# Two early weight slabs, states in a kept order, and scaled tiles evicted by ACT

## The chip, the cores and the metric

The kernel runs on one core of a Trainium2 chip. The metric is device time in microseconds of one execution; lower is better. The engines that matter are PE (TensorE, matrix products), DVE (VectorE), ACT (ScalarE), POOL (GpSimd) and SP (SyncE, which here only issues DMAs). Each works through its own list of instructions in order; semaphores make one engine wait for another.

## The reference

One inference step of one hybrid decoder layer, for a prompt of 512 positions and 8 samples of 4 positions, all in float32:

```
n = RMSNorm(h);  z = n @ w_in            # q | k | v | gate | gMLP u | v | branch gates A | B
q, k = rotary(q), rotary(k) * DK**-0.5   # 4 heads, DK 256, DV 512
o, s_new = retention_chunked(q, k, v, s0)
y_a = silu(gate) * rmsnorm(o, g_ret)     # the norm is by head
y_b = gelu(u) * spatial_gating(layernorm(gelu(v)))
h = h + (sigmoid(zga) * (y_a @ w_br_a) + sigmoid(zgb) * (y_b @ w_br_b)) @ w_o
h = h + square(relu(rmsnorm(h) @ w_up)) @ w_down
h = h + sigmoid(rmsnorm(h) @ w_pg) * (p @ w_pp)
```

The outputs are the normed h of all positions, the new retention states of prompt and samples, and the samples' gMLP rows.

## The kernel before

Activations lie transposed: a tile has 128 features as partitions and 544 columns (512 prompt positions, 32 sample positions). A weight slab is 128 x 1024 float32, 512 KB, and holds what one tile of 128 output features needs (8 blocks of 128 x 128).

Float32 products are made of three products of a cheaper type. `split` writes a value's high part (`hi`, a cast on ACT, L123) and its remainder (`lo`, a subtraction on DVE, L124, which reads `hi`). Weights and activations are both split, and a block's product is hi·hi + hi·lo + lo·hi. `dense` (L304) issues a tile's products: 8 blocks, 3 products, 2 halves of 272 columns, 48 matmuls into one `Product`, a pair of PSUM banks called `f`. There are two such pairs, used in turn, so a tile's first matmul waits until the tile two before it has been read out of PSUM.

`Feed` brings the weights. A list of jobs is planned beforehand; `load` issues slab loads on SP while one of 4 raw buffers is free, and `wide` splits a raw slab into one of 3 `hl` buffers. The first two slabs come differently: `begin(2)` sets them aside and `piece(i)` loads them in quarters between the 8 loads of the input `xT`, so that PE can start early.

Head 0 makes the query tiles q0 and q1 together (`first_two`), from activations scaled by the norm's weights but not yet by 1/rms, because the rms is not known yet. The squares (L473) and their sum (L474), kept in program order by `pin`, give `r1`. `copied` takes a product out of PSUM by ACT (L602). `times_r1` takes it out by DVE and multiplies by `r1` on the way (L596); it serves the two key tiles k0, k1 and the first two value tiles v0, v1 of head 0. From v2 on the activations themselves are normalised (L619, eight tiles, split again), so plain copies do. Then come v3 and four gate tiles. Heads 1 to 3 have the same tiles, and between a head's keys and values stands the branch-A product of the head before (`branch_a`, `ya` being its gated and normed output: `group_normed`, the multiplication in L880 and then a split).

Around the dense tiles lies the attention work of the head as small "chores" that fall due some ticks later: key and value transposes on PE (`kt`, `vt`, and `vs` for the sample rows, fed by a copy on POOL, L900), scores, `state_ahead` (loads a sample's 256 x 512 state by SP, L806, into one of 5 buffers, and splits it), `sample_state` (products with it), `prompt_output`, `group_norm` (a ones-product on PE, a square root on ACT, a reciprocal on DVE, L491).

The order of each engine's instructions is not the order of the code. A scheduler goes through a modelled timeline when the program is built and fixes one list for each engine; instructions under `pin` keep their order among themselves. At run time nothing overtakes.

Of the kernel before, what the change touches and what calls it, by code (L numbers as in the profile page):

```python
# [11 lines left out]
ALU = mybir.AluOpType  # L12
# [45 lines left out]
class Slots:  # L58
# [11 lines left out]
    def get(self, dtype=F32):  # L70
        i = self.free.popleft()
        self.count += 1
        t = self.pools[i].tile([P, T], dtype, tag=f"s{i}", name=f"s{i}_{self.count}")
        self.where[id(t)] = (i, t)
        return t
# [7 lines left out]
def halves(ap):  # L83
    return ap.rearrange("p (a b) -> p a b", a=2)


def layer(tc, a, o):
    nc = tc.nc
    act, dve, pool, pe = nc.scalar, nc.vector, nc.gpsimd, nc.tensor
    with ExitStack() as ctx:  # L90
# [9 lines left out]
        get, put = slots.get, slots.put  # L100
# [21 lines left out]
        def split(hi, lo, src):  # L122
            act.copy(hi, src)  # L123
            dve.tensor_tensor(out=lo, in0=src, in1=hi.bitcast(F32), op=ALU.subtract)  # L124

        class Feed:
# [35 lines left out]
            def piece(self, i):  # L162
                c, d = (slice(i * SLAB // 4 + e, (i + 1) * SLAB // 4 + e) for e in (0, SLAB))
                for t, hl, src in self.first:
                    nc.sync.dma_start(t[:, c], src[:, c])
                for t, hl, src in self.first:
                    split(hl[:, c], hl[:, d], t[:, c])
                if i == 3:
                    self.busy -= len(self.first)

            def load(self):
                while self.jobs:
# [101 lines left out]
        feed = Feed()  # L274
# [8 lines left out]
        def bank(name="m"):  # L283
            return psm[-1].tile([P, 512], F32, tag="m", name=name)
# [28 lines left out]
        def tile_of(xs):  # L313

            w = feed.take()
            ps = Product()
            dense(ps, [(*at(w, k * P), *xs[k]) for k in range(KD)])
            return ps
# [147 lines left out]
        pin = tc.keep_in_program_order  # L466
# [27 lines left out]
        def scaled_split(src, g):  # L494

            hi, lo = get(F32R), get(F32R)
            act.activation(hi, src, AF.Copy, scale=g)
            dve.scalar_tensor_tensor(
                out=lo, in0=src, scalar=g, in1=hi.bitcast(F32), op0=ALU.mult, op1=ALU.subtract
            )  # L500
            return hi, lo
# [48 lines left out]
        ps = bank("warm")  # L550
# [5 lines left out]
        def g(base, k):  # L556
            return gcols[:, base + k : base + k + 1]
# [3 lines left out]
        for k in range(KD):  # L561
            t = get()
            nc.sync.dma_start(t, a["xT"][k * P : (k + 1) * P, :])
            xs_raw.append(t)
            xs.append(scaled_split(t, g(G_MIX, k)))
            if k % 2 == 0:
                feed.piece(k // 2)
        total = get()
        for k in range(KD):
            add_square(total, xs_raw[k], k == 0, pin)  # L570
# [13 lines left out]
        r1s = {}  # L584
# [7 lines left out]
            return tile_of(xs)  # L592

        def times_r1(ps):
            t = get()
            dve.tensor_tensor(out=halves(t), in0=ps.all, in1=halves(r1s["r"]), op=ALU.mult)  # L596
            return t


        def copied(ps):  # L600
            t = get()
            act.copy(halves(t), ps.all)  # L602
            return t
# [197 lines left out]
        def state_ahead(c, b):  # L801

            km = hp.tile([96, DK], F32R, tag="km", name="km", bufs=2)
            act.activation(km, c.k3.bitcast(F32), AF.Copy, scale=maskb[:, b : b + 1])  # L804
            raw = hp.tile([P, 2, DV], F32, tag="state", name="state", bufs=STATES)
            nc.sync.dma_start(raw, a["state"][b, c.h].rearrange("(i p) v -> p i v", i=2))  # L806
            parts = []
            for i in range(2):
                hi, lo = get(F32R), get(F32R)
                split(hi[:, :DV], lo[:, :DV], raw[:, i])  # L810
                parts.append((hi, lo))
            c.states[b] = km, raw, parts
# [75 lines left out]
        def values(c):  # L888
            c.vh = hp.tile([P, 4, DV], F32R, tag="vh", name="vh")
            c.vl = hp.tile([P, 4, DV], F32R, tag="vl", name="vl")  # L890
            c.pvs = bank("vs")
            for m2 in range(2):
                if c.h == m2 == 0:
                    t2 = [times_r1(next_in()) for _ in range(2)]
                    renew()
                else:
                    t2 = pair()
                for i, t in enumerate(t2):
                    r = hp.tile([P, 96], F32, tag="v96", name="v96", bufs=2)
                    pool.tensor_copy(  # L900
                        r.rearrange("p (a s) -> p a s", a=3), t[:, None, LP:].to_broadcast([P, 3, NS])
                    )
                    later(VALUES[i], lambda m=2 * m2 + i, t=t, r=r: values_by_token(c, m, t, r))
# [14 lines left out]
        for h in range(H):  # L918
            c = Head()
            c.h = h  # L920
            head_tables(c)
            r = None
            if h == 0:
                q = [copied(ps) for ps in first_two(xs, [(k,) for k in range(KD)])]
                start_norm()
                r = r1s["r"]
                chores([(2 * j, normalise, j) for j in range(KD)])
                k = [times_r1(next_in()) for _ in range(2)]
            else:
                q = pair()  # L930
                k = pair()
# [17 lines left out]
            for b in range(NB):  # L949
                plan += [(AHEAD[b], state_ahead, c, b), (STATE[b], sample_state, c, b)]  # L950
# [185 lines left out]
        for m in range(KD):  # L1136
            ps, t = tile_of(yb), get()
# [163 lines left out]
        for s in range(2):  # L1301
# [3 lines left out]
            for i in range(0, KD, 2):  # L1305
# [15 lines left out]
                t, sq = get(), get()  # L1321
# [5 lines left out]
                for j, (t1, sq1, m) in enumerate(x2):  # L1327
                    for c0, c1 in quarters[2:] if end and j else ((s * TH, (s + 1) * TH),):
                        c, p = slice(c0, c1), slice(c0 - s * TH, c1 - s * TH)
                        if end:  # L1330
                            ps = todo[0] if j else area
# [16 lines left out]
                else:  # L1348
                    dve.tensor_tensor(
                        out=squares[:, :TH], in0=squares[:, :TH], in1=squares[:, TH:], op=ALU.add  # L1350
# [140 lines left out]
```

## Time and profile before

| what | value |
|---|---|
| median of 3 runs | 1263.17 us (1261.87 to 1264.41) |
| the profiled execution, its own time | 1260.18 us |
| its span, first to last instruction | 1258.4 us |
| PE busy, of the span | 98% |
| DVE, ACT, POOL busy | 70%, 50%, 7% |
| mean granted clock of PE | 0.996 |
| DMA | 176.27 MB, 140 GB/s on average |

The profile gives, for one execution, the busy time of each engine, who waited for whom, and the instructions in order of time. A row of the timeline reads: start, length, engine and line, operation, tile written <- tiles read, count, and in brackets the idle time before it and what ended that. Rows that follow each other with the same work are merged ("x48"). Matmuls are pipelined: one lasts 0.289 us in the records, and the next starts about 0.127 us after it. SP rows are DMA issues, not transfers.

### The profile page before, as it was taken

To read this page: it belongs to the slowest core of one execution; us is meant where nothing else is said; L and a number is where in the kernel's file an instruction comes from. 1 tells how busy PE (TensorE), PEld (TensorE's weight loads), DVE (VectorE), ACT (ScalarE), POOL (GpSimd) and SP (SyncE) were. 2 spreads that over 40 slices of the span, in tenths; PEclk is the share of its full clock that TensorE was granted. 3 is DMA by queue.
4 is the path that set the end of the run, shared out by engine and by line. 5 is a ranking of instruction groups with operands and counts; after the bars stand their busy time and mean duration, and the time that the engine had idled before them with its cause. 6 is when DMAs were issued, how large, how long until landed. Compare 5 with 4: busy or idle time off the path is not lost.

```text
span 1258.4 us, 22939 instructions
## 1 busy us (share of the span) xinstructions
PE 1236.8 (98%) x9432; PEld 1206.0 (96%) x9432; DVE 887.0 (70%) x1297; ACT 630.3 (50%) x1047; POOL 92.6 (7%) x127
## 2 busy tenths in 40 slices
PE   8999999999999999999999999999999999999996
PEld 8989999999999998999999999999999999999995
DVE  7976854686468655767678654559459879888966
ACT  6453553443434353643455532446248568577733
POOL 0201100110010001010000000000000001000000
PEclk9999999999999999999999999999999999999998
DMA  9328323822263225653546453222546667665302
GB/s 313 112 94 273 104 78 103 280 92 87 92 247 122 85 70 202 212 160 92 129 135 187 141 202 93 85 84 91 127 114 162 173 173 180 186 163 149 122 18 71
DMA packets 65336, 176.27 MB, mean 140 GB/s; under 512 B 7408, under 2 KB 10736, under 8 KB 65232
## 3 DMA queue, kind: packets, MB, share of 16 engines
q1 hardware_dynamic: 54288, 135.42, 32.6%
q0 software_dynamic: 10944, 39.39, 13.4%
q8 instruction: 74, 1.21, 0.4%
q14 instruction: 30, 0.25, 0.1%
HBM read 153.55 MB, written 21.23 MB: 139 GB/s over the span
## 4 chain that ended last, share of the span: by engine, by line
PE 53%; DVE 2%; ACT 2%; DMA 1%; issue 0%; DVEq 0%; ACTq 0%
PE f L304 20%; PE fa L390 16%; PE f L390 12%; PE pg L304 4%; DVE hl L124 1%; PE sp L1081 1%; ACT hl L123 1%; DMA raw<-in_w_down 0%; PE norm L486 0%; DVE s L491 0%; DVE s L124 0%; DMA raw<-in_w_pg 0%; PE sp L1082 0%; PE gt L968 0%; DVE s L880 0%
## 5 line engine op out<-in xcount | busy, mean ns | idle before, releaser
L304 PE MATMUL f<-s,hl 128*128 128x272 f32 x5088 | 674.0, 289 | 4.5 <-ACT hl L123 1.8
L304 PEld LDWEIGHTS f<-s,hl 128*128 128x128 f32 x5088 | 655.2, 188 | 12.5 <-ACT hl L123 2.2
L124 DVE TENSOR_TENSOR hl<-raw,hl 128x1024 fp32r<-128x1024 f32 (+2 forms) x259 | 288.8, 1123 | 107.3 <-ACT hl L123 105.1
L123 ACT CAST hl<-raw 128x1024 fp32r<-128x1024 f32 (+2 forms) x259 | 249.1, 969 | 177.2 <-PE f L304 99.0
L390 PE MATMUL fa<-s,hl 128*128 128x272 f32 x1728 | 238.9, 289 | 2.0 <-ACT hl L123 1.0
L390 PEld LDWEIGHTS fa<-s,hl 128*128 128x128 f32 x1728 | 224.3, 188 | 4.2 <-ACT hl L123 1.6
L390 PE MATMUL f<-s,hl 128*128 128x272 f32 x1296 | 183.5, 288 | 1.7 <-DVE s L409 1.1
L390 PEld LDWEIGHTS f<-s,hl 128*128 128x128 f32 x1296 | 170.1, 188 | 3.1 <-DVE s L409 2.0
L123 ACT CAST s<-s 128x544 fp32r<-128x544 f32 (+4 forms) x170 | 97.4, 598 | 48.0 <-DVE s L765 12.2
L124 DVE TENSOR_TENSOR s<-s,s 128x544 fp32r<-128x544 f32 (+4 forms) x170 | 108.6, 659 | 6.4 <-ACT s L123 5.7
L826 DVE SCALAR_TENSOR_TENSOR state<-state,su 128x512 f32<-128x512 f32 x64 | 43.8, 685 | 38.1 <-PE su L825 38.0
L123 ACT CAST s<-state 128x512 fp32r<-128x512 f32 x64 | 37.9, 621 | 38.4 <-DMA state<-in_state 18.7
L124 DVE TENSOR_TENSOR s<-state,s 128x512 fp32r<-128x512 f32 x64 | 42.8, 687 | 19.8 <-ACT s L123 16.7
L417 ACT ACTIVATE s<-fa 128x272 f32<-128x272 f32 x36 | 14.3, 398 | 64.5 <-PE fa L390 64.5
L602 ACT COPY s<-f 128x544 f32<-128x544 f32 x28 | 17.2, 614 | 48.8 <-PE f L304 48.6
L491 DVE RECIPROCAL s<-s 128x544 f32<-128x544 f32 (+1 forms) x9 | 28.6, 3176 | 10.0 <-ACT s L489 10.0
L193 POOL DMA_DIRECT2D raw<-in_w_up x12 | 10.3, 854 | 311.3 <-DVE s L124 189.4
L304 PE MATMUL pg<-s,s 128*128 128x272 f32 x240 | 30.7, 288 | 0.0
L804 ACT ACTIVATE km<-k,maskb 96x256 fp32r<-96x256 f32 x32 | 15.9, 508 | 29.3 <-PE su L825 28.6
L830 POOL DMA_DIRECT2D out_state_s<-state x32 | 23.0, 719 | 101.2 <-DVE state L826 101.2
L304 PEld LDWEIGHTS pg<-s,s 128*128 128x128 f32 x240 | 30.3, 188 | 0.1
L464 PE MATMUL o<-s,vh 128*128 128x256 f32 (+2 forms) x128 | 30.3, 324 | 0.0
(179 smaller groups left out, 1128.7 us busy)
## 6 DMA issues: line engine op xcount, KB each, us to landing
raw<-in_w_in SPq DMA_DIRECT2D x66, 512.0 KB, 3.3
state<-in_state SPq DMA_DIRECT2D x32, 512.0 KB, 4.8
out_state_s<-state POOLq DMA_DIRECT2D x32, 512.0 KB, 4.7
raw<-in_w_up SPq DMA_DIRECT2D x20, 512.0 KB, 3.3
raw<-in_w_down SPq DMA_DIRECT2D x20, 512.0 KB, 3.3
raw<-in_w_in SPq DMA_DIRECT2D x36, 256.0 KB, 3.2
raw<-in_w_up SPq DMA_DIRECT2D x36, 256.0 KB, 3.3
raw<-in_w_down SPq DMA_DIRECT2D x36, 256.0 KB, 3.4
```

The costliest lines, as they stand in the source:

```text
L123: act.copy(hi, src)
L124: dve.tensor_tensor(out=lo, in0=src, in1=hi.bitcast(F32), op=ALU.subtract)
L304: pe.matmul(ps.p[s], w, x[:, s * TH : (s + 1) * TH], start=first and i == 0 and j == 0, stop=last and i == n - 1 and j == 2, skip_group_ch ...
L390: pe.matmul(ps, a_, b_, start=first and k == j == 0, stop=k == 3 and j == 2, skip_group_check=True)
L417: act.activation(t1[:, hi_half], pa, AF.Copy, scale=-1.0)
L464: pe.matmul(ps[:rows, c], u, v, start=i == 0 and j == 0, stop=i == n - 1 and j == 2)
L491: dve.reciprocal(r[:, c], r[:, c])
L602: act.copy(halves(t), ps.all)
L804: act.activation(km, c.k3.bitcast(F32), AF.Copy, scale=maskb[:, b : b + 1])
L826: dve.scalar_tensor_tensor(out=raw[:, i], in0=raw[:, i], scalar=gamma**LS, in1=ps, op0=ALU.mult, op1=ALU.add)
L830: pool.dma_start(o["state_s"][b, c.h].rearrange("(i p) v -> p i v", i=2), raw)
L1081: pe.matmul(ps[:, j * P : (j + 1) * P], gvt[j][m // 4][:, cols], wst[:, m], start=True, stop=True)
```

## The change

Three edits. First, a new method `begun` is called when the input loads have all been issued: it runs `load` at once, so two more slabs (the third and fourth, for k0 and k1) are asked for on SP ahead of the tables (`cos`, `sin`, five small ones, `dtab`, `qmask`). Only then are the first two raw buffers given back; `piece` no longer does this. Second, the state loads of head 0 are put under `pin`. Third, `times_r1` takes the product out of PSUM by ACT (`copied`) and multiplies by `r1` in SBUF on DVE.

```diff
                 for t, hl, src in self.first:
                     split(hl[:, c], hl[:, d], t[:, c])
-                if i == 3:
-                    self.busy -= len(self.first)
+
+            def begun(self):
+
+                self.load()
+                self.busy -= len(self.first)
...
             if k % 2 == 0:
                 feed.piece(k // 2)
+        feed.begun()
         total = get()
...
         def times_r1(ps):
-            t = get()
-            dve.tensor_tensor(out=halves(t), in0=ps.all, in1=halves(r1s["r"]), op=ALU.mult)
+            t = copied(ps)
+            dve.tensor_tensor(out=t, in0=t, in1=r1s["r"], op=ALU.mult)
             return t
...
-            nc.sync.dma_start(raw, a["state"][b, c.h].rearrange("(i p) v -> p i v", i=2))
+            load = nc.sync.dma_start(raw, a["state"][b, c.h].rearrange("(i p) v -> p i v", i=2))
+            if c.h == 0:
+                pin(load)
```

The lists of the engines that the scheduler makes of this differ up to the scores of head 1, some 1200 matmuls in; from there on they hold the same instructions in the same order. Line numbers of the new kernel are 3 to 5 higher. Three places matter for what follows.

SP, at the start. `s` tiles filled from `in_xT` are the input, `raw` of 128x1024 a whole slab. Before:

```order
L563 DMA s_22_164<-in_xT 128x544
L572 DMA s_33_193<-in_cos 128x544
L573 DMA s_34_194<-in_sin 128x544
L580 DMA st_dec<-in_st_dec 128x16
L580 DMA sts<-in_sts 96x4
L580 DMA maskb<-in_maskb 96x8
L580 DMA dsam<-in_dsam 96x128
L580 DMA fold<-in_fold 64x32
L665 DMA dtab<-in_dtab 128x640
L667 DMA qmask<-in_qmask 128x256
L185 DMA raw<-in_w_in 128x1024 x4
L806 DMA state<-in_state 128x2x512 x5
```

Now:

```order
L188 DMA raw<-in_w_in 128x1024 x2
L576 DMA s_33_197<-in_cos 128x544
L577 DMA s_34_198<-in_sin 128x544
L584 DMA st_dec<-in_st_dec 128x16
L584 DMA sts<-in_sts 96x4
L584 DMA maskb<-in_maskb 96x8
L584 DMA dsam<-in_dsam 96x128
L584 DMA fold<-in_fold 64x32
L668 DMA dtab<-in_dtab 128x640
L670 DMA qmask<-in_qmask 128x256
L188 DMA raw<-in_w_in 128x1024 x11
L809 DMA state<-in_state 128x2x512 x2
```

Two slabs moved ahead of nine tables, and the five first states moved from behind the sixth slab of the kernel to behind the fifteenth and later.

ACT, from the last square of the first norm on. `s_35` and `s_36` are q0 and q1 out of PSUM, `s_42` and `s_47` are k0 and k1, `s_37` is r1, and each cast to `hl` is the high part of the next slab. Before:

```order
L473 ACTIVATE s_32_190<-s_22_164 128x544
L602 COPY s_35_327<-f 128x544
L123 CAST hl<-raw 128x1024
L602 COPY s_36_329<-f 128x544
L123 CAST hl<-raw 128x1024 x2
L489 ACTIVATE s_37_331<-norm,eps 128x272 x2
L123 CAST hl<-raw 128x1024
L123 CAST s_38_351<-s_1_98 128x544
L123 CAST s_40_380<-s_4_110 128x544
L123 CAST hl<-raw 128x1024
```

Now:

```order
L476 ACTIVATE s_32_194<-s_22_164 128x544
L123 CAST hl<-raw 128x1024
L605 COPY s_35_327<-f 128x544
L123 CAST hl<-raw 128x1024
L605 COPY s_36_329<-f 128x544
L123 CAST hl<-raw 128x1024
L492 ACTIVATE s_37_331<-norm,eps 128x272 x2
L605 COPY s_42_408<-f 128x544
L123 CAST hl<-raw 128x1024
L123 CAST s_38_351<-s_1_98 128x544
L123 CAST s_40_380<-s_4_110 128x544
L605 COPY s_47_475<-f 128x544
```

The third slab's cast moved ahead of the copy of q0, and the copies of k0 and k1 are new. On DVE the multiplications of k0, k1, v0, v1 stand where they stood.

ACT, at the keys of head 1. `s_137` and `s_143` are its query tiles, `s_148` and `s_149` its keys k0 and k1; `s_139`, `s_141`, `s_144`, `s_146` are the high parts of `ya` of head 0, which PE reads in the first product after k1 (`branch_a`). Before:

```order
L123 CAST s_139_1532<-s_103_999 128x544
L123 CAST s_141_1549<-s_113_1131 128x544
L123 CAST s_144_1574<-s_128_1279 128x544
L123 CAST s_146_1591<-s_133_1381 128x544
L602 COPY s_148_1631<-f 128x544
L123 CAST hl<-raw 128x1024
L123 CAST s_161_1819<-s_137_1491 128x544
L123 CAST s_163_1824<-s_143_1565 128x544
L123 CAST s_166_1829<-s_165_1828 128x8x32
L602 COPY s_149_1687<-f 128x544
L123 CAST hl<-raw 128x1024
```

Now:

```order
L605 COPY s_148_1635<-f 128x544
L123 CAST hl<-raw 128x1024
L123 CAST s_163_1828<-s_143_1569 128x544
L123 CAST s_166_1833<-s_165_1832 128x8x32
L605 COPY s_149_1691<-f 128x544
L123 CAST hl<-raw 128x1024
L123 CAST s_139_1536<-s_103_1003 128x544
L123 CAST s_141_1553<-s_113_1135 128x544
L123 CAST s_144_1578<-s_128_1283 128x544
L123 CAST s_146_1595<-s_133_1385 128x544
```

The four casts of `ya` moved from ahead of the copy of k0 to behind the copy of k1 and one slab's cast.

DVE, at the same place. `s_138` is 1/rms of the group norm, made by the reciprocal; `s_140`, `s_142`, `s_145`, `s_147` are the low parts of `ya`. Before:

```order
L491 RECIPROCAL s_138_1499<-s_138_1499 128x544
L634 TENSOR_TENSOR s_158_1770<-s_143_1565,s_34_194 128x544
L880 TENSOR_TENSOR s_103_999<-s_103_999,s_138_1499 128x544
L880 TENSOR_TENSOR s_113_1131<-s_113_1131,s_138_1499 128x544
L880 TENSOR_TENSOR s_128_1279<-s_128_1279,s_138_1499 128x544
L880 TENSOR_TENSOR s_133_1381<-s_133_1381,s_138_1499 128x544
L124 TENSOR_TENSOR hl<-raw,hl 128x1024
L635 TENSOR_TENSOR s_143_1565<-s_143_1565,s_33_193 128x544
L636 TENSOR_TENSOR s_137_1491<-s_137_1491,s_158_1770 128x544
L124 TENSOR_TENSOR s_140_1533<-s_103_999,s_139_1532 128x544
```

Now, the reciprocal standing six instructions ahead of the first row:

```order
L885 TENSOR_TENSOR s_103_1003<-s_103_1003,s_138_1503 128x544
L885 TENSOR_TENSOR s_113_1135<-s_113_1135,s_138_1503 128x544
L885 TENSOR_TENSOR s_128_1283<-s_128_1283,s_138_1503 128x544
L885 TENSOR_TENSOR s_133_1385<-s_133_1385,s_138_1503 128x544
L686 TENSOR_TENSOR s_167_1837<-qs,qmask 128x256
L124 TENSOR_TENSOR s_164_1829<-s_143_1569,s_163_1828 128x544
L124 TENSOR_TENSOR s_166_1833<-s_165_1832,s_166_1833 128x8x32
L636 TENSOR_TENSOR s_148_1635<-s_148_1635,s_33_197 128x544
L637 TENSOR_TENSOR s_150_1699<-s_149_1691,s_34_198 128x544
L124 TENSOR_TENSOR hl<-raw,hl 128x1024
L124 TENSOR_TENSOR s_140_1537<-s_103_1003,s_139_1536 128x544
```

Between the reciprocal and the first low part of `ya` stood 8 instructions, 1 of them on a slab; now 15 stand there: 2 of them are on slabs, and 3 read k0 or k1.

PE's list at that place has the 48 matmuls of k1 and then, with nothing between, the products with `s_139`, then `s_140`. In head 0, PE's transposes of v0 and v1 (`vt`, `vs`) stood 12 and 45 matmuls into v2 (the first `vs` 18); now they stand 4 and 25 matmuls into v3.

## The prediction

> **What bounds the kernel.** I read the page's busy shares first, then busy times by stretch, then who waited for whom, then the timeline at the places that the new lists touch.
>
> ```profile
> PE 1236.8 (98%) x9432; PEld 1206.0 (96%) x9432; DVE 887.0 (70%) x1297; ACT 630.3 (50%) x1047; POOL 92.6 (7%) x127
> ```
>
> PE is busy 98% of the span. The change neither adds nor removes a matmul, so it can only win what PE idles in the stretch it touches, and lose by making PE idle anew.
>
> ```profile
> 20.00:25.00 5.00, 3.58 (x26) 3.37 (x27) 4.13 (x5) 3.49 (x4) 0.00 (x0) 1.00 0.97 366
> ...
> 40.00:50.00 10.00, 8.73 (x68) 8.34 (x67) 10.00 (x16) 3.25 (x4) 1.62 (x1) 1.00 0.16 52
> 50.00:60.00 10.00, 9.74 (x78) 9.28 (x77) 10.00 (x16) 5.20 (x9) 6.91 (x7) 1.00 0.31 107
> 60.00:80.00 20.00, 20.00 (x157) 19.65 (x156) 17.48 (x32) 13.87 (x26) 0.97 (x2) 1.00 0.23 73
> 80.00:100.00 20.00, 20.00 (x118) 16.68 (x117) 11.45 (x18) 5.99 (x11) 3.82 (x6) 1.00 0.53 174
> 100.00:120.00 20.00, 20.00 (x133) 18.38 (x132) 14.30 (x21) 8.57 (x16) 3.59 (x5) 1.00 0.83 268
> ```
>
> Columns: stretch, length, then busy us of PE, weight loads, DVE, ACT, POOL, then PE's granted clock, DMA share, GB/s. PE loses 1.4 us in 20 to 25 and 1.5 us in 40 to 60, where DVE is full (10.00 of 10) and ACT half empty; from 60 on it loses nothing.
>
> ```profile
> PE f L304 <- ACT hl L123: 1.8, 2, 1.6
> ...
> PE f L304 <- DVE s L596: 1.3, 2, 0.7
> ```
> ```profile
> L777 PE MATMUL vs<-ident,v 128*96 128x128 f32 x16 | 4.4, 278 | 0.3
> ```
>
> The waits are those the edits aim at: a slab's cast, and `times_r1` on DVE (L596). 0.3 us more are `vs` transposes waiting for POOL's copy of v.
>
> **The change, part by part.** Idle time counts from the modelled end of the last matmul, 0.29 us after its start, while the next would normally start after 0.13: each gap costs 0.16 more than it shows.
>
> *Early slabs.*
>
> ```profile
> 14.92 3.94 ACT L473 ACTIVATE s<-s 128x544 f32<-128x544 f32 x7
> 15.59 4.87 DVE L474 TENSOR_TENSOR s<-s,s 128x544 f32<-128x544 f32 x6 [0.29 <-ACT s L473]
> 15.88 1.86 SPq L185 DMA_DIRECT2D raw<-in_w_in  x4
> ...
> 18.75 0.59 ACT L602 COPY s<-f 128x544 f32<-128x544 f32 x1
> 19.83 1.04 ACT L123 CAST hl<-raw 128x1024 fp32r<-128x1024 f32 x1 [0.48 <-DMA raw<-in_w_in]
> ...
> 20.91 1.23 DVE L124 TENSOR_TENSOR hl<-raw,hl 128x1024 fp32r<-128x1024 f32 x1 [0.44 <-ACT hl L123]
> 20.93 0.77 PE L304 MATMUL f<-s,hl 128*128 128x272 f32 x4 [1.61 <-ACT hl L123]
> ...
> 22.19 3.17 PE L304 MATMUL f<-s,hl 128*128 128x272 f32 x23 [0.49 <-DVE hl L124]
> ```
>
> The slab now lands well before ACT is through its squares, so the DMA wait is gone. But ACT still ends the squares first: cast 18.8 to 19.8, then the copy of q0 to 20.4, which k0 needs as well, since it takes q0's place in PSUM. PE can start k0 at 20.45. After 4 matmuls it needs `lo`, and DVE's six additions last until 20.46: `lo` ends at 21.65 instead of 22.15. PE's fifth matmul comes at 21.65 instead of 22.19: **0.54 us won**, not the 2.4 us of both gaps. Bounds: 0 and 2.4. The tables land later by two slabs' time; the first is read by rotary, behind eight normalisations, so that costs nothing while DVE is this late.
>
> *Eviction by ACT.*
>
> ```profile
> 41.61 6.28 PE L304 MATMUL f<-s,hl 128*128 128x272 f32 x48 [0.70 <-DVE s L596]
> ...
> 48.38 3.10 POOL L900 COPY v<-s 128x96 f32<-128x96 f32 x1 [47.00 <-DVE s L596]
> 48.46 1.76 PE L304 MATMUL f<-s,hl 128*128 128x272 f32 x12 [0.57 <-DVE s L596]
> ...
> 52.05 3.71 POOL L900 COPY v<-s 128x96 f32<-128x96 f32 x1 [0.57 <-DVE s L596]
> ```
>
> v1 and v2 waited 0.70 and 0.57 us for PSUM that DVE had not yet read. ACT's copies stand right behind k0, k1, v0, v1, a tile of 6.2 us ahead of need: 0.70 + 0.57 + 2 x 0.16 = **1.6 us won**. The cost is four copies of 0.6 us on ACT, hidden in its 11 idle us between 40 and 60; DVE multiplies as often as before. The two `vs` waits (0.3 + 0.3) go too, because these transposes now stand a tile later, while v0 and v1 are multiplied where they were: **0.6 us won**. Bounds: 0 and 2.2 together.
>
> *States kept in order.* Their splits leave DVE's full stretch for 60 to 120, where it has 17 idle us. I cost it at nothing; the cover is quoted with the third rival.
>
> *What the moved lists cost.* Now the place where I expect the loss, the first product of branch A.
>
> ```profile
> 128.34 27.82 PE L304 MATMUL f<-s,hl 128*128 128x272 f32 x218
> ...
> 129.26 3.55 DVE L491 RECIPROCAL s<-s 128x544 f32<-128x544 f32 x1 [0.94 <-ACT s L489]
> ...
> 132.00 0.62 ACT L602 COPY s<-f 128x544 f32<-128x544 f32 x1 [2.77 <-PE f L304]
> 132.51 1.05 ACT L123 CAST hl<-raw 128x1024 fp32r<-128x1024 f32 x1
> 132.73 0.66 DVE L634 TENSOR_TENSOR s<-s,s 128x544 f32<-128x544 f32 x1
> 133.31 2.62 DVE L880 TENSOR_TENSOR s<-s,s 128x544 f32<-128x544 f32 x4
> 134.06 2.55 ACT L123 CAST s<-s 128x544 fp32r<-128x544 f32 x4 [0.49 <-DVE s L880]
> 135.84 1.22 DVE L124 TENSOR_TENSOR hl<-raw,hl 128x1024 fp32r<-128x1024 f32 x1
> ...
> 138.25 2.63 DVE L124 TENSOR_TENSOR s<-s,s 128x544 fp32r<-128x544 f32 x4
> ...
> 142.25 0.43 DVE L683 TENSOR_TENSOR s<-qs,qmask 128x256 f32<-128x256 f32 x1
> ```
>
> Before, `ya` was cast (134.06) two tiles ahead of its use, and PE ran through without a gap. Now ACT must first copy k1, which exists only when PE has finished the tile directly ahead of that product. Let C be the start of ACT's copy of q1. PE makes k0 and k1 in 2 x 48 x 0.127 us plus a norm product of 0.3: k1's copy starts at C + 12.5, and undisturbed PE would be 0.2 us into the next product. ACT then copies (steps from start to start: 0.51), casts a slab (0.95) and casts `ya` (0.65): C + 14.6, so even the high part is 2.3 us late. The low part is later still. From C, DVE waits for the copy (0.65), does three rotary steps (2.05) and a slab (1.14), and starts the reciprocal at C + 3.85. Up to the end of the first low part follow reciprocal 3.47, ten 128x544 at 0.64, three 128x256 at 0.35, two slabs at 1.14, and 0.72: 13.9 us, so C + 17.75. PE's fifth matmul, due at C + 12.8, comes at C + 17.8: **5.0 us lost**. Were DVE not behind, it would still need ACT's slab cast (C + 14.1), its own slab step (1.14) and 0.72, C + 16.0: 3.2 us lost, the lower bound; the upper, with POOL's copy of the queries, which one of the small steps reads, as slow as its slowest row (3.7), is some 6 (an estimate). I take 5.0, since all its steps have rows.
>
> *The clock.* That is 5.2 us in which PE runs four matmuls.
>
> ```profile
> 1244.00:1246.00 2.00, 0.96 (x9) 0.77 (x7) 1.34 (x5) 1.15 (x4) 0.00 (x0) 1.00 0.00 0
> 1246.00:1248.00 2.00, 0.50 (x3) 0.30 (x3) 0.97 (x4) 1.29 (x2) 0.00 (x0) 1.00 0.00 0
> 1248.00:1250.00 2.00, 0.94 (x6) 0.72 (x6) 0.70 (x3) 0.64 (x2) 0.00 (x0) 0.80 0.00 0
> 1250.00:1252.00 2.00, 0.00 (x0) 0.00 (x0) 1.96 (x3) 0.00 (x0) 0.00 (x0) 0.50 0.00 0
> ```
> ```profile
> 1.16 5.49 PE L552 MATMUL warm<-ones 128*128 128x128 f32 x24 [1.16 <-DVE ones L549]
> ...
> 50.06 0.60 PE L776 MATMUL vt<-ident,s 128*128 128x128 f32 x4
> ```
>
> At the kernel's end the granted clock fell to 0.50 near 1249, after some 4 us in which PE was busy under half the time; the 2.1 us idle out of 3 at 19.3 to 22.2 did not lower it. The new stall is emptier and longer than the end's, so I expect the clock to fall there. A slow clock's price: the first 24 passes took 0.21 us each (5.49 less the last one's length), the four at 50.06 about 0.11, so PE was at half speed for some 5 us at the start, a loss of 2.6. If the clock falls in mid-stall, 2.5 us of that are idle anyway: 1.3. I take the middle, **1.9 us lost**; bounds 0 and 2.6.
>
> The Trainium skill, "TensorE: Matmul & The Clock Gate", section "What's actually happening", says that the clock halves after an idle window of 3.4 us in a free-running count, and comes back after a busy one. The rows above agree that it falls. Taken strictly, a whole window must lie in the stall without the four matmuls counting, which the window's phase decides from run to run; a busy window at half clock would lose 1.7 us, and my estimate by that page is a sum 0.2 us lower, or 1.9 lower where no window fits.
>
> **The sum.** -0.54 - 1.6 - 0.6 + 5.0 + 1.9 = +4.2 us. Against the profiled execution's 1260.18 that is 1264.4. The median of the runs is 1263.17, 3.0 higher, so I forecast **1267.4**.
>
> **Rivals.** First, the clock holds. Everything turns on one figure, PE's share of work in the stall, against the share at which the clock falls. For it: it held through the gaps near 20 us. Against: the end of the kernel. It gives -2.7 + 5.0 = +2.3, 1265.5; with the stall at its least, +0.5, 1263.7, so not slower within the 0.2% (2.5 us) that a measurement of this kernel can tell from no change; with the whole slab gap won as well, -1.4.
>
> Second, the wait at branch A does not stand, because PE comes there late enough for other reasons, or the group norm runs earlier than I place it. That leaves -2.7: 1260.5, faster. Against it: ACT's list puts copy and slab cast behind k1's end whatever the clock of the other engines.
>
> Third, the states come too late.
>
> ```profile
> 87.96 0.39 PE L822 MATMUL so<-s,s 128*64 128x512 f32 x1
> ```
> ```profile
> state<-in_state SPq DMA_DIRECT2D x32, 512.0 KB, 4.8
> ```
>
> PE first reads a state near 88. The first states stand behind the fifteenth slab, which takes the raw buffer of the eleventh; that is cast when v3 is done, two tiles of 6.3 us after v2's start at 48.46, so near 61. A state lands 4.8 us after its issue, and its splits follow; some 20 us are to spare. But SP issues in order: a kept state that waits for a buffer holds the slabs behind it, and PE with them. One such wait of about 2 us would give +6.2: 1269.4.
>
> Fourth, the early slabs do nothing, since squares and additions bind: +4.7, 1267.9, inside the first case.
>
> **How the numbers follow.** Stall and slow clock 0.50, of which 0.44 slower and 0.06 same; its own range 1265.8 to 1269. Clock holds 0.30: 0.07 slower, 0.22 same, 0.01 faster. No wait 0.10: 0.08 faster, 0.02 same. Late states or another new wait 0.10, slower. Together faster 0.09, same 0.30, slower 0.61. The range 1262.4 to 1269.2 leaves out most of the second rival, the far end of the third, and the least stall with the largest gains.
>
> **What would show it.** Right: the slab cast starts right after the squares, with PE idle in two pieces of about 1.1 and 0.5 us; no gap at v1 and v2; then at about 140 us two gaps of 2 to 2.5 us in the first product after head 1's keys, the first ended by ACT's cast, the second by DVE's low part; a granted clock under 1 for some us behind them. Wrong: no gap there, or PE idle between 60 and 130 us for states; a clock of 1.00 throughout would take 1.9 us off.

## The result: 0.7% slower, twice the loss that was forecast

| kernel | median | ratio to before, 95% interval |
|---|---|---|
| before | 1263.79 us (4 runs) | |
| changed | 1273.30 us (1271.37 to 1274.12, 4 runs) | 1.0072 [1.0051, 1.0094] |
| changed, a second time | 1271.83 us (4 runs) | 1.0065 [1.0047, 1.0082] |

The forecast was 1267.4, from 1262.4 to 1269.2: slower, as it came, but by 4.2 us where 8.4 to 9.5 were measured. The profiled execution took 1274.12 us, its span 1272.4.

The page's busy line first: the work is the same, and PE does it in a longer span.

```profile
PE 1241.5 (98%) x9432; PEld 1210.3 (95%) x9432; DVE 886.9 (70%) x1297; ACT 630.2 (50%) x1051; POOL 91.6 (7%) x127
```

The stretches that were shown of the kernel before, with the columns as there (PE, weight loads, DVE, ACT, POOL, granted clock, DMA):

```profile
20.00:25.00 5.00, 3.95 (x28) 3.71 (x29) 3.54 (x4) 2.42 (x4) 0.00 (x0) 1.00 0.91 284
...
40.00:50.00 10.00, 10.00 (x82) 10.00 (x82) 10.00 (x16) 3.13 (x4) 1.08 (x1) 1.00 0.16 55
50.00:60.00 10.00, 6.59 (x43) 6.36 (x42) 8.57 (x12) 2.04 (x3) 8.78 (x6) 0.78 0.46 157
60.00:80.00 20.00, 20.00 (x149) 19.64 (x148) 13.07 (x23) 12.42 (x23) 1.18 (x3) 0.94 0.43 145
...
140.00:160.00 20.00, 15.48 (x101) 15.05 (x101) 17.96 (x26) 8.45 (x14) 2.29 (x4) 0.83 0.24 83
```

The 1.3 us of idle between 40 and 50 are gone, as forecast. But there are two holes of 3.4 and 4.5 us, at 50 to 60 and at 140 to 160, and the granted clock is below 1 in and behind both. PE's own waits name them:

```profile
PE vs L780 <- POOL v L905: 3.4, 1, 3.4
PE f L307 <- DVE s L124: 2.3, 1, 2.3
PE f L307 <- ACT s L123: 2.2, 1, 2.2
```

The second and third are the stall at branch A that the prediction described. The first is where it had booked a gain. The timeline of the changed kernel around it (L905 is POOL's copy of the sample rows, L780 the `vs` transpose, L600 the multiplication by r1):

```profile
48.14 0.71 DVE L600 TENSOR_TENSOR s<-s,s 128x544 f32<-128x544 f32 x1
48.77 1.21 DVE L124 TENSOR_TENSOR hl<-raw,hl 128x1024 fp32r<-128x1024 f32 x1
48.92 8.12 POOL L905 COPY v<-s 128x96 f32<-128x96 f32 x2 [47.54 <-DVE s L600]
...
51.18 0.71 DVE L600 TENSOR_TENSOR s<-s,s 128x544 f32<-128x544 f32 x1
51.82 1.21 DVE L124 TENSOR_TENSOR hl<-raw,hl 128x1024 fp32r<-128x1024 f32 x1
...
55.49 1.22 DVE L124 TENSOR_TENSOR hl<-raw,hl 128x1024 fp32r<-128x1024 f32 x1
56.63 0.68 DVE L124 TENSOR_TENSOR vl<-vt,vh 128x512 fp32r<-128x512 f32 x1
...
56.89 0.45 PE L780 MATMUL vs<-ident,v 128*96 128x128 f32 x1 [3.41 <-POOL v L905]
```

The copy of v0's 96 columns starts at 48.92 and holds PE up until 56.89. Everything that DVE runs from 48.92 on reads two tiles in SBUF, the memory that holds `s`, `raw` and `hl` (`s<-s,s`, `hl<-raw,hl`); the first instruction with an operand in PSUM, where PE's products `f` and `vt` lie, is the low part of a transposed tile, `vl<-vt,vh`, at 56.63, and the copy is through a quarter of a microsecond later. In the kernel before, where the copies took 3.10 us (from 48.38) and 3.71 us (from 52.05), DVE's rows read:

```profile
50.63 0.72 DVE L633 TENSOR_TENSOR s<-s,s 128x544 f32<-128x544 f32 x1
51.27 0.72 DVE L596 TENSOR_TENSOR s<-f,s 128x544 f32<-128x544 f32 x1
...
55.54 0.70 DVE L124 TENSOR_TENSOR vl<-vt,vh 128x512 fp32r<-128x512 f32 x1
```

48.38 + 3.10 is 51.48, 0.21 us after a multiplication out of PSUM (`s<-f,s`) began; 52.05 + 3.71 is 55.76, 0.22 us after `vl<-vt,vh` began. The change turned the multiplication of v1 from `s<-f,s` into `s<-s,s`, and with it went the opening that POOL's copy had used.

### The profile page after: what moved, and what is told of

Its sections match the earlier page's. It is cut to its first block, busy times and chain, and to the rows that moved or that the text cites. A ratio compares the mean times of both kernels' runs of the same rounds, so it can differ in the third digit from the quotient of the medians.

```text
span 1272.4 us, 22937 instructions
## 1 busy us (share of the span) xinstructions
PE 1241.5 (98%) x9432; PEld 1210.3 (95%) x9432; DVE 886.9 (70%) x1297; ACT 630.2 (50%) x1051; POOL 91.6 (7%) x127
## 4 chain that ended last, share of the span: by engine, by line
PE 89%; DVE 6%; DMA 2%; ACT 2%; issue 1%; POOL 1%; SPq 0%; DVEq 0%; ACTq 0%
PE f L307 47%; PE fa L393 15%; PE f L393 11%; PE pg L307 4%; PE o L467 2%; PE st L467 2%; DVE hl L124 2%; PE sc L467 1%; PE su L830 1%; PE so L827 1%; PE so L828 1%; DVE s L124 1%; DMA s<-in_xT 1%; PE norm L489 1%; DMA s<-in_pT 1%
## 5 line engine op out<-in xcount | busy, mean ns | idle before, releaser
L124 DVE TENSOR_TENSOR hl<-raw,hl 128x1024 fp32r<-128x1024 f32 (+2 forms) x259 | 289.0, 1123 | 119.3 <-ACT hl L123 117.1
L123 ACT CAST s<-s 128x544 fp32r<-128x544 f32 (+4 forms) x170 | 96.7, 596 | 55.8 <-DVE s L768 13.9
L124 DVE TENSOR_TENSOR s<-s,s 128x544 fp32r<-128x544 f32 (+4 forms) x170 | 108.3, 656 | 6.3 <-ACT s L123 5.3
L124 DVE TENSOR_TENSOR s<-state,s 128x512 fp32r<-128x512 f32 x64 | 42.6, 686 | 20.3 <-ACT s L123 17.3
L605 ACT COPY s<-f 128x544 f32<-128x544 f32 x32 | 19.6, 613 | 63.6 <-PE f L307 63.5
```

## Which edit brings the loss

Four runs split the change. Their edits are hunks of the diff that was shown.

**e1, the third edit alone, put into the kernel before:**

```diff
-            t = get()
-            dve.tensor_tensor(out=halves(t), in0=ps.all, in1=halves(r1s["r"]), op=ALU.mult)
+            t = copied(ps)
+            dve.tensor_tensor(out=t, in0=t, in1=r1s["r"], op=ALU.mult)
```

> The kernel before with the third edit alone: times_r1 copies the product out of PSUM by ACT and multiplies in SBUF. Theory: the whole loss comes from this edit, in two places. (1) Between v0's multiplication and the first transposed value tile DVE then runs only instructions that read two SBUF tiles, and POOL's copy of v0's sample rows does not get through: PE idles 3 to 4 us at the first vs. (2) The order at branch A of head 1 turns, so PE idles about 2.2 + 2.3 us there. The granted clock falls to 0.5 for 6.8 us behind each. The time is that of the changed kernel plus the 0.5 us of the early slabs: about 1273.8, +9 to +10 on before. Rival: the early slabs or the kept states carry a part (later input, states behind the fifteenth slab): then this run is 1270 or less.

Measured: 1272.93 us, ratio 1.0074 [1.0057, 1.0091]. The gap at the first `vs` is 4.0 us, those at branch A 2.2 and 2.0. The clock behind the first gap was at half for 3.4 us, not 6.8.

**e2, the changed kernel with that hunk undone:**

> The changed kernel without the third edit: two early slabs and kept states only, times_r1 on DVE from PSUM as before. Theory: about 1263.3, 0.5 us under before; the two waits for PSUM at v1 and v2 (0.70 and 0.57 us) are back, the branch A product of head 1 starts without a gap, the granted clock is 1.00 from 20 us to the end of the kernel, and PE does not idle for states between 60 and 130 us. Rival: the early slabs delay the input and the states come late, worth 1 to 3 us: 1265 to 1267.

Measured: 1262.46 us, 0.9993 [0.9983, 1.0004]. The waits at v1 and v2 are back (0.72 and 0.61 us), there is no gap at branch A. One thing came otherwise: the granted clock fell to 0.5 for 3.4 us near 22 (below).

**e9 and e10, the early slabs alone (`feed.begun()`) and the kept states alone (`pin(load)`), each put into the kernel before:**

> The kernel before with the first edit alone: two slabs asked for ahead of the tables. Theory: 0.5 us under before, about 1263, with the wait for the slab's cast near 20 us shorter by half a microsecond and the two waits for PSUM at v1 and v2 as before. The granted clock falls near 22 us in some executions and not in others, as the place of its window has it. On the wait for in_pT near 1110 (open so far): if the eviction edit brings it, it lands within 4.5 us of its issue here and PE does not idle there; if it is chance, it can take 6 us and more here too.

> The kernel before with the second edit alone: head 0's state loads kept in program order. Theory: no change, within 0.1% of before; PE does not idle for states between 60 and 130 us. Rival (kept states hold the slabs behind them): 2 us or more slower, with PE waiting for a slab's cast between 60 and 130 us. in_pT: as in the run beside it, landing within 4.5 us if its lateness belongs to the eviction edit.

Measured: 1262.52, 0.9989 [0.9974, 1.0003], and 1262.62, 0.9992 [0.9981, 1.0002]. Both may be worth the half microsecond or nothing; neither loses. With kept states PE is busy 80.00 us of the 80 between 60 and 140. So the whole loss comes from the eviction, and it brings both places.

The wait for in_pT (the second input, read near 1110) was a suspect for a further loss. ACT waited 4.32 us for it in the changed kernel and PE idled some 2 us there; before, ACT waited 0.30. The same rows of the changed kernel and then of e9, which has no eviction edit:

```profile
1116.33 1.33 ACT L123 CAST s<-s 128x544 fp32r<-128x544 f32 x2 [4.32 <-DMA s<-in_pT]
```
```profile
1107.97 0.64 ACT L123 CAST s<-s 128x544 fp32r<-128x544 f32 x1 [4.30 <-DMA s<-in_pT]
```

So the late landing does not need the eviction. Still, ACT waited 2.4 to 4.3 us in all for in_pT in each of the nine profiles with it, and as long in only one of the four without (before, e2, e9, e10). What decides it was not settled.

## The two places, mended one by one

**e3, the sample columns of v0 and v1 copied by ACT:**

```diff
-                    pool.tensor_copy(
+                    (act.copy if c.h == m2 == 0 else pool.tensor_copy)(
```

> The changed kernel, with the copies of the sample columns of v0 and v1 of head 0 done by ACT instead of POOL. Theory (POOL is kept out by DVE's two-operand SBUF instructions): the 3.4 us gap at the first vs goes, and with it the first stretch at half clock (56 to 62 us), 3.4 + 0.16 + 2.75 = 6.3 us: about 1267.0. The gaps at branch A stay. Rival (v0 itself is ready too late on DVE, or the transposes stand too early): the gap stays at 2 us or more with ACT as the one waited for, and the time stays over 1271.

Measured: 1266.24 us, 1.0022 [1.0013, 1.0031], 5.6 and 7.1 us under the two medians of the changed kernel, where 6.3 were expected. The hole at 50 to 60 is gone and that at branch A is not:

```profile
50.00:60.00 10.00, 10.00 (x83) 10.00 (x82) 10.00 (x16) 4.31 (x8) 4.23 (x4) 1.00 0.50 157
...
140.00:160.00 20.00, 15.81 (x102) 15.01 (x101) 15.46 (x26) 9.99 (x18) 2.02 (x3) 0.83 0.27 85
```

**e4, DVE's multiplications by the group norm kept ahead of head 1's rotary (`keep` is `pin` for head 0, and for head 1's rotary of the queries):**

```diff
-            dve.tensor_tensor(out=t, in0=t, in1=c.ro, op=ALU.mult)
+            keep(dve.tensor_tensor(out=t, in0=t, in1=c.ro, op=ALU.mult))
...
-            dve.tensor_tensor(out=d, in0=o1, in1=sin, op=ALU.mult)
+            keep(dve.tensor_tensor(out=d, in0=o1, in1=sin, op=ALU.mult))
...
```

> The changed kernel, with DVE's four multiplications by the group norm of head 0 kept in program order with head 1's rotary of the queries, as they stood before the change. POOL copies as in the changed kernel. Theory (branch A waits only because DVE multiplies and ACT casts stand behind the keys of head 1): the gaps of 2.2 and 2.3 us at branch A go, but for some 0.4, and the second stretch at half clock (151 to 158 us) goes too: 4.8 + 2.76 - 0.4 = 7.2 us less, about 1266.1. The 3.4 us gap at vs and its half clock stay. Rival (PE would wait there for the slabs or the scores just the same): 1271 or more.

Measured: 1265.17 us, 1.0009 [0.9999, 1.0019], 6.7 and 8.1 us under the two medians of the changed kernel, where 7.2 were expected. Here the hole at 50 to 60 stays, and 140 to 160 is full:

```profile
50.00:60.00 10.00, 6.59 (x53) 6.35 (x52) 9.96 (x14) 2.05 (x3) 9.40 (x3) 0.98 0.40 133
...
140.00:160.00 20.00, 19.79 (x158) 19.58 (x158) 17.77 (x24) 9.62 (x15) 0.89 (x2) 1.00 0.27 94
```

**e5, the changed kernel again, and e6, both mends together:**

> The changed kernel once more, as the base for the three beside it. Theory: about 1273, +9 to +10 on before; the two gaps of 3.4 us or more at vs and of 2.2 + 2.3 us at branch A stand in any execution, while the length of each stretch at half clock (3.4 or 6.8 us) may differ, since it goes by a window whose place differs from execution to execution. The wait of ACT for in_pT near 1110 (4.3 us in the first profile) is open: 2 us or more again if it comes with the change, under 0.5 us as before the change if it is chance.

> The changed kernel with both mends: sample columns of v0 and v1 copied by ACT, and DVE's four multiplications by the group norm kept ahead of head 1's rotary of the queries. Theory: the two places are independent, so that the gains add: 1273.3 - 6.7 - 7.8 = 1258.8 by the two runs that mend one each; by the terms of the sum that are left (0.5 of the slab, 1.6 of the waits at v1 and v2, 0.6 at vs, less 0.3 at branch A) 2.4 us under before, 1261. So 1258.8 to 1261, faster than both kernels, with no gap over 0.4 us between 25 and 500 us and the clock at 1.00 there. Rival: the eviction edit brings a further loss that neither mend reaches (the longer wait for in_pT): 1262 to 1264, no better than before.

Measured: e5 1271.83, as above. e6 **1260.33 us, 0.9971 [0.996, 0.9982]**: faster than both kernels by 3.1 and 11.5 us, and within the 1258.8 to 1261 expected. Its clock did fall once, at 538, in a gap of 2.1 us that is 0.8 in the profile of before; between 25 and 500 it was 1.00.

The gains add, as a count by place shows. For each profile, the time from the 130th to the 400th and from there to the 1080th PE instruction, by the starts in the records:

| kernel | 130 to 400 (holds v0 to v3) | 400 to 1080 (holds branch A) |
|---|---|---|
| before | 36.57 us | 96.01 us |
| changed | 40.06 | 104.05 |
| e3, copy on ACT | 34.09 | 103.22 |
| e4, norm kept | 40.32 | 96.42 |
| e6, both | 34.11 | 96.50 |

## Is it DVE's operands that keep POOL out?

**e7, v1 alone multiplied out of PSUM again:**

```diff
-                    t2 = [times_r1(next_in()) for _ in range(2)]
+                    t2 = [times_r1(next_in()), times_r1_psum(next_in())]
```

> The changed kernel, with v1 of head 0 alone multiplied by DVE straight out of PSUM as before the change; k0, k1, v0 go by ACT. POOL's copies stay on POOL. Theory (POOL gets through only beside a DVE instruction that does not read two SBUF tiles): POOL's copy of v0 ends with the multiplication of v1 out of PSUM, near 51 us, after some 2.5 us instead of 7.9; PE's gap at the first vs goes, with its half clock: about 1267. Rival (POOL's copies are slow by themselves there, or wait for a pause of DVE): DVE runs through as before, so the copy still lasts until 56 or so and PE idles 3 us or more.

Measured: 1268.69 us, 1.0041 [1.0024, 1.0058], 3.1 and 4.6 us under the two medians of the changed kernel, where about 1267 was expected. DVE runs through without a pause (L605 is v1's multiplication here):

```profile
51.79 1.83 POOL L910 COPY v<-s 128x96 f32<-128x96 f32 x1 [50.41 <-DVE s L600]
52.78 0.71 DVE L642 TENSOR_TENSOR s<-s,s 128x544 f32<-128x544 f32 x1
53.42 0.71 DVE L605 TENSOR_TENSOR s<-f,s 128x544 f32<-128x544 f32 x1
...
54.19 5.72 POOL L910 COPY v<-s 128x96 f32<-128x96 f32 x2 [0.57 <-DVE s L605]
...
59.50 1.27 DVE L124 TENSOR_TENSOR vl<-vt,vh 128x512 fp32r<-128x512 f32 x2
59.76 0.32 PE L785 MATMUL vs<-ident,v 128*96 128x128 f32 x1 [0.86 <-POOL v L910]
```

v0's copy ends at 53.62, 0.20 us into the instruction that reads PSUM: 1.83 us in place of some 7.9. v1's copy then waits for the next such instruction, at 59.50, so a gap of 0.86 is left at the second `vs`. So one multiplication out of PSUM let one copy through, and only that one.

**e11, one needless DVE instruction that reads a single SBUF tile:**

```diff
+                    dve.tensor_scalar(out=t2[1], in0=t2[1], scalar1=1.0, scalar2=None, op0=ALU.mult)
```

> The changed kernel, with one needless DVE instruction more: v1's tile multiplied by 1.0 in place, which reads one SBUF tile only (128x544). On DVE it stands one slab step (1.2 us) ahead of the first low part of a transposed value tile. Theory (only two SBUF operands at once keep POOL out): POOL's copy of v0 ends with this instruction, 1.5 to 2 us earlier than the first low part, and PE's gap at the first vs is that much shorter, 1.5 to 2 us instead of 3.4. Rival (any DVE instruction on SBUF keeps POOL out, only one that reads PSUM lets it in): the copy still ends with the first low part of a transposed tile, and the gap is 3.4 us or more. No time is asked of this run.

```profile
50.60 8.26 POOL L906 COPY v<-s 128x96 f32<-128x96 f32 x1 [49.23 <-DVE s L600]
...
57.17 0.45 DVE L900 TENSOR_SCALAR s<-s 128x544 f32<-128x544 f32 x1
...
58.65 0.69 DVE L124 TENSOR_TENSOR vl<-vt,vh 128x512 fp32r<-128x512 f32 x1
...
58.92 0.32 PE L780 MATMUL vs<-ident,v 128*96 128x128 f32 x1 [3.76 <-POOL v L906]
```

A single execution took 1272.02 us. Here my theory fell: the single-operand instruction let nothing through, and the copy ended at 58.86, again 0.21 us after the low part began. So it isn't two operands as such. Nor is it any SBUF operand: in the changed kernel POOL's copy of the queries ends at 138.77, 0.15 us into the reciprocal, which reads one SBUF tile too, but slowly.

```profile
137.73 1.04 POOL L677 COPY qs<-s 128x32 f32<-128x32 f32 x1 [11.52 <-DVE s L639]
138.62 3.54 DVE L494 RECIPROCAL s<-s 128x544 f32<-128x544 f32 x1
```

What fits the rows so far: two SBUF inputs keep POOL's copy out, and so does one that is read fast (0.45 us for 128x544); a PSUM operand or a slow single input lets it in.

It is not the whole rule. These rows are of e4 (L642, L124 and L688 follow each other on DVE without a pause):

```profile
161.78 0.72 DVE L642 TENSOR_TENSOR s<-s,s 128x544 f32<-128x544 f32 x1
161.92 0.64 POOL L679 COPY qs<-s 128x32 f32<-128x32 f32 x1 [8.45 <-DVE s L641]
162.41 1.23 DVE L124 TENSOR_TENSOR hl<-raw,hl 128x1024 fp32r<-128x1024 f32 x1
162.55 1.16 POOL L679 COPY qs<-s 128x32 f32<-128x32 f32 x1
163.56 0.43 DVE L688 TENSOR_TENSOR s<-qs,qmask 128x256 f32<-128x256 f32 x1
```

The copies end at 162.56 and 163.71, each 0.15 us into an instruction with two SBUF inputs; e6 shows the same. What let these two in is not shown. e3 shows that the gap at `vs` hangs on POOL's copy, and e7 that a PSUM operand of DVE frees it; which instructions let POOL in, in general, stays open.

The Trainium skill, "SBUF — State Buffer", section "Who interferes with whom", says that DVE and GpSimd share one pair of ports, that a DVE instruction with two SBUF inputs contends with a GpSimd one that reads SBUF, that a tensor_scalar can run in a mode that takes the pair as well, and that the later one blocks fully. The rows agree on who keeps whom out, e11's and the reciprocal's too; that e11's instruction ran in that mode is read from its 0.45 us alone. They differ on how long: e4's two copies waited for one DVE instruction each, but the changed kernel's copy of v0 sat through nine that started after it.

## The slow clock

**e8, the stall at branch A filled with four needless products:**

```diff
             if before is not None:
+                if h == 1:
+                    fill = bank("warm")
+                    for _ in range(4):
+                        pe.matmul(fill, ident, k[1][:, :512], start=True, stop=True)
                 branch_a(before.h, before.ya)
```

> The changed kernel, with four needless float32 products of 128x512 (some 3.5 us of PE) placed in the stall ahead of branch A's first product in head 1; nothing waits for them and they leave time for the data. Theory (the clock falls since PE is too little busy in some 3.4 us): the granted clock stays at 1.00 at 140 to 165 us, the stall itself is as long as before, and the time falls by the 2.76 us that half the clock cost: about 1270.5. Rival (the clock falls for another reason, or the loss behind the stall is not the clock): 1273 or more, with the clock at 0.5 behind the stall or not.

Measured: 1269.86 us, 1.0051 [1.0031, 1.0071], against 1271.83 for e5 on the same chip, where 1270.5 was expected. The fill lies inside the stall, and the clock holds (the row of the fill, then the stretch):

```profile
146.98 3.70 PE L947 MATMUL warm<-s,ident 128*128 128x512 f32 x8 [0.70 <-ACT s L605]
```
```profile
140.00:160.00 20.00, 18.91 (x124) 16.31 (x124) 18.47 (x29) 10.55 (x18) 2.29 (x4) 1.00 0.20 67
```

From the 400th to the 1080th PE instruction it takes 101.59 us, the fill not counted, against 104.05 and 104.03: the slow clock behind the stall costs 2.45 us. The figure is taken at this place alone, since the profile of e8 has no fall at `vs` either, by the place of the grid described below.

The profile of the changed kernel, cut at the times at which its clock changed, shows when it falls and comes back (granted clock is the column behind POOL's):

```profile
52.14:55.56 3.42, 1.34 (x12) 1.10 (x10) 3.42 (x6) 2.04 (x3) 3.42 (x1) 1.00 0.55 207
55.56:58.97 3.41, 2.08 (x10) 2.09 (x11) 3.02 (x5) 0.00 (x0) 2.98 (x5) 0.50 0.39 139
58.97:62.38 3.41, 3.41 (x17) 3.41 (x17) 0.00 (x0) 0.00 (x0) 0.24 (x2) 0.50 0.08 30
62.38:65.80 3.42, 3.42 (x29) 3.42 (x28) 2.41 (x5) 1.68 (x3) 0.00 (x0) 1.00 0.00 0
```

The clock changes on a grid of 3.413 us. A window in which PE loaded weights for only 1.10 us is followed by half the clock; a window with a hole of 1.3 us does not end that, a full one does. How full it must be, other profiles bound: a window at half clock with 2.94 us of PE ended it (e9, 21.80 to 25.21), one with 2.87 did not (e7, 21.20 to 24.62), though it held more weight loads (2.74 against 2.64).

## Why the prediction was wrong, step by step

- **The step that failed:** "The two `vs` waits (0.3 + 0.3) go too, because these transposes now stand a tile later, while v0 and v1 are multiplied where they were: 0.6 us won." The 0.6 did go, but a gap of 3.41 us came, 3.57 with the 0.16 by which a gap costs more than it shows; less the 0.6, that is 3.0 us lost instead of 0.6 won. The step compared positions and took the length of POOL's copies, 3.10 and 3.71 us in the quoted rows, as fixed. That a copy of 96 columns takes 3 us at all was the sign left unread: its length was a wait for DVE, and the edit took away what ended it. The sentence "DVE multiplies as often as before" was true and beside the point, since what the multiplications read had changed.
- **A second clock fall follows from it,** 6.8 us in the first profile, of which PE idled 1.33: (6.83 - 1.33) / 2 = 2.75 us lost. In e5 it lasted 3.4 us.
- **Stall at branch A, +5.0:** 2.19 + 2.32 + 2 x 0.16 = 4.83, first ended by ACT's cast, then by DVE's low part, as forecast. e4 shows it to be the order alone. The two waits:

```profile
149.35 0.77 PE L307 MATMUL f<-s,hl 128*128 128x272 f32 x4 [2.19 <-ACT s L123]
152.44 7.75 PE L307 MATMUL f<-s,hl 128*128 128x272 f32 x40 [2.32 <-DVE s L124]
```

- **Clock behind it, +1.9:** it fell; 2.45 by e8. A little under-sized, within the bounds of 0 and 2.6. The argument for its rival, that the clock held through the gaps near 20 us, rested on the luck of one execution: between 21 and 25 us it fell in eight of the 13 profiles.
- **Waits at v1 and v2, -1.6:** gone. e2 has them back.
- **Early slabs, -0.54:** the two gaps near 20 were 1.06 and 0.55 where before had 1.61 and 0.49, so 0.5 in this pair:

```profile
20.51 0.77 PE L307 MATMUL f<-s,hl 128*128 128x272 f32 x4 [1.06 <-ACT s L605]
21.82 2.39 PE L307 MATMUL f<-s,hl 128*128 128x272 f32 x17 [0.55 <-DVE hl L124]
```

  It drowns in how executions differ there: the first gap was 3.73 us in e10.
- **States, nothing:** e10 agrees.
- **Range and rivals:** "another new wait" had a chance of 0.10 together with late states, and the range ended at one of 2 us. Added up with what was found, the steps give -0.5 - 1.6 + 3.0 + 2.75 + 4.83 + 2.45 = 10.9 us for the first profile, against 13.9 between the two profiled executions. The rest is about what was lost where in_pT landed late: from the 8100th to the 9000th PE instruction the changed kernel took 120.49 us, before 117.60. The medians lie only 8.4 to 9.5 apart, since the profiled execution of before (1260.18) was among its fastest.

## What to carry to other kernels

Where an instruction takes ten times as long as its twins elsewhere, its length is likely a wait, as it was here: find what ended it before you move work around it. An eviction that moves a DVE operand from PSUM to SBUF is not free when POOL works beside it, even if DVE's time stays the same; a short copy that PE waits for was better placed on an idle ACT here. And when a scheduler sets the order, read the new lists beyond the place of the edit: half of this loss lay a head later, and a few kept instructions gave it back.

## What the hardware showed that was not expected

In its long copies POOL did not get a turn between two DVE instructions with SBUF inputs: what takes 0.26 us elsewhere lasted up to 8.52 (e1) while DVE started ten of them. In the 13 profiles all 18 copies of v that lasted over 1.8 us ended 0.20 to 0.23 us after the start of a DVE instruction that reads PSUM. Shorter copies got their turn sooner, as e4's did.

The clock goes by a share, not by full idleness. Cutting 13 profiles into windows of 3.413 us on the grid of their clock changes, all 33 windows at full clock in which weight loads filled 1.38 us or less were followed by half the clock, and none with 1.54 us or more. Two that lie close together, of e2 and of e8 (weight loads are the second busy time, behind PE's), with the window behind each:

```profile
18.45:21.86 3.41, 1.79 (x13) 1.35 (x12) 3.20 (x5) 3.14 (x5) 0.00 (x0) 1.00 0.80 239
21.86:25.28 3.42, 3.42 (x18) 3.42 (x17) 1.54 (x3) 1.05 (x1) 0.00 (x0) 0.50 0.92 333
```
```profile
56.65:60.06 3.41, 1.56 (x13) 1.56 (x14) 3.41 (x5) 0.00 (x0) 3.11 (x3) 1.00 0.39 117
60.06:63.47 3.41, 3.41 (x31) 3.41 (x30) 1.07 (x3) 1.55 (x3) 0.77 (x4) 1.00 0.26 103
```

The Trainium skill, "TensorE: Matmul & The Clock Gate", section "What's actually happening", gives a free-running window of 3413 ns, and the grid agrees. A strictly idle window isn't needed. Since the grid lies differently in each execution, gaps of 1.08 and 0.54 us near 20 cost the clock in e2, and 1.61 and 0.49 did not in the profile of before; e8's gap of 3.4 us at `vs`, cut in half by the grid, cost none.
